# Low parts of the weights on GpSimd in pieces of 256 columns, none from C's last gates to the merge, and two one-column products with pointer scalars

## The chip, the cores and the metric

The kernel runs on one core of a Trainium2 chip. The metric is the device time of one execution in microseconds (us). The engines are called as the profile calls them: PE is TensorE (PEld its weight loads), DVE is VectorE, ACT is ScalarE, POOL is GpSimd, and SP is SyncE, which issues the DMA transfers.

## The reference

A bidirectional encoder trunk of two layers for 512 positions of width 1024, all in float32. Each layer normalises its input, projects it once, and feeds three token mixers: A (grouped attention with axial rotary positions), B (differential attention) and C (multi-head latent attention). Their outputs are merged by gates, projected and added back. A squared-ReLU MLP of width 4096 follows.

```python
for l in range(DEPTH):
    p = _split_columns(rms_norm(x, ln1) @ w_in[l])        # A, B, C and three gates of 1024 columns
    ys = gqa_axial(...), diff_attention(...), mla(...)    # 512 columns each
    merged = sum(sigmoid(gate[n]) * (ys[n] @ w_branch[l, n]) for n in range(3))
    x = x + merged @ w_out[l]
    x = x + relu(rms_norm(x, ln2) @ w_ff1[l]) ** 2 @ w_ff2[l]
return rms_norm(x, final_g)

# inside diff_attention, for each head: two softmaxes and
p = p[0] - lam * p[1]
```

## The kernel before

Every large product is made of three products of split operands. A weight tile of 128 rows and up to 1024 columns comes from memory raw (`wr`). ACT rounds it to the high part `wh` (L60), and DVE or POOL makes the low part `wl` = raw - high (L63). TensorE then multiplies high by high, high by low and low by high; of a weight tile, each 128 columns serve one step of the accumulation, with its three products one behind the other. There are two buffers of raw tiles (`NWR`) and three each of high and low parts (`NW`). A raw tile is free for SyncE's next fetch when its low part is made. All low parts count up `nw`, and `nw % 5 < POOLW` sends one to POOL, else to DVE:

```python
e = t.nc.gpsimd if t.nw % 5 < t.POOLW else t.nc.vector
e.tensor_tensor(wl, self.raw, wh.bitcast(F32), op=ALU.subtract)
```

`POOLW` is 1 (`P0`) from a layer's start, 5 (`PA`) from A's attention on, so that all low parts are POOL's, and 0 (`PF`) from `stat2`, which is called in the first MLP product once output products and their sums are made.

`Trunk.plan` lists a layer's work as (cost, function, weights). `run` goes through that list, fetches weights 8 plan-us ahead (`AHEAD_F`) and splits them 3 plan-us ahead (`AHEAD_S`). `weave` spreads filling work (projections, gates, branch products) between the units of an attention by their costs; `defer` and `tick` call follow-up steps (transposes, products with the values) when a due time on the plan's clock has come. So a low part stands in its engine's queue where the plan's clock put it, and each engine runs its queue in order.

The stages of layer 0 in the trace, in us from the span's start: start and A's projection 0 to 65, A's attention 65 to 180 (with B's projections as filler), B's 180 to 300 (with gates and branch products of A), C's projection 300 to 360, C's attention 360 to 543, the merge 543 to 571, the output product 571 to 613, and the MLP 613 to 963. Layer 1 repeats them from 963 on, and the last norm ends at 1929.

The places that matter below:

- `probs` makes a 128 x 512 block of scores, takes the row maximum (L512, `mx`), in A and C scales it with `scale`, a 128 x 1 column (L516), and lets ACT make the exponential (L517). B's probabilities combine two of them: the second sum's reciprocal (L672) is multiplied by the negated lambda `nlam` and the first sum (L673, both 128 x 1), and L674 adds the two blocks.
- `rsqrt` (L169 to L180) is a chain of small DVE operations; L621 adds the halves of a rotated B block, and L784 makes a part of C's rotated key.
- `branch` (L920, L922) of the third mixer scales a gate `gc`, adds it to the running sum `mg` on DVE, and splits the sum into high (ACT, L150) and low part (DVE, L157): the merged tile `mp`, from which `out` is multiplied. For the second mixer L922 runs on POOL.
- L528 transposes the probabilities on PE, and L532 takes their low part. L155 and L157 make low parts of activations.

Of the kernel before, what the change touches and what calls it, by code (L numbers as in the profile page):

```python
# [10 lines left out]
F32 = mybir.dt.float32  # L11
# [3 lines left out]
ALU = mybir.AluOpType  # L15
# [26 lines left out]
class Weight:  # L42
# [11 lines left out]
    def get(self):  # L54
        if self.parts is None:
            self.fetch()
            t = self.t
            wh = t.p.tile([128, self.cols], F32R, tag="wh", name="wh", bufs=t.NW)
            wl = t.p.tile([128, self.cols], F32R, tag="wl", name="wl", bufs=t.NW)
            t.nc.scalar.copy(wh, self.raw)  # L60
            t.nw += 1
            e = t.nc.gpsimd if t.nw % 5 < t.POOLW else t.nc.vector
            e.tensor_tensor(wl, self.raw, wh.bitcast(F32), op=ALU.subtract)  # L63
            self.parts = wh, wl
        return self.parts


class Trunk:
# [24 lines left out]
    def run(self, plan):  # L93

        at, ws = 0.0, []
        for c, _, w in plan:
            ws += [(at, x) for x in w]
            at += c
        t0, kf, kg = self.t, 0, 0
        for c, f, _ in plan:  # L100
            now = self.t - t0
            while kf < len(ws) and ws[kf][0] <= now + self.AHEAD_F:
                ws[kf][1].fetch()
                kf += 1
            while kg < len(ws) and ws[kg][0] <= now + self.AHEAD_S:
                ws[kg][1].get()
                kg += 1
            self.tick(self.t)
            f()
            self.t += c  # L110

    @staticmethod
    def weave(att, fill):

        tf = sum(x[0] for x in fill)
        done, k, r = 0.0, 0, []
        for i, a in enumerate(att):
            r.append(a)
            while k < len(fill) and done + fill[k][0] / 2 <= tf * (i + 1) / len(att):
                r.append(fill[k])  # L120
                done += fill[k][0]
                k += 1
        return r + fill[k:]
# [382 lines left out]
    def probs(self, mms, scale=None, z=None):  # L506

        nc = self.nc
        s = self.ps("S", "sc")
        self.mm(s, mms)  # L510
        m = self.small("mx", 1, 8)
        nc.vector.tensor_reduce(m, s, axis=AX.X, op=ALU.max, negate=True)  # L512
        p = self.p.tile([128, 512], F32, tag="p", name="p", bufs=self.NP)
        z = self.small("z", 1, 8) if z is None else z
        if scale is not None:
            nc.vector.tensor_tensor(m, m, scale, op=ALU.mult)  # L516
        nc.scalar.activation(p, s, AF.Exp, bias=m, scale=1.0 if scale is None else scale, accum_out=z)  # L517
        return p, z

# [56 lines left out]
    def att_a(self):  # L576
        self.y = {}

        def probs(h, qt):
            g, j, e = h // 4, h // 2, h % 2  # L580
            q = slice(qt * 128, (qt + 1) * 128)
            G, K = self.want(self.aG, j), self.want(self.aK, g)
            i = qt * 4 + h % 4
            p, z = self.probs([(G[:, e, q], K[:, 0]), (G[:, e, q], K[:, 1])], self.aR[g][:, i : i + 1])
            self.normalise(p, z)
            return p

        def vt(h):
            o = 64 * (h % 2)
            return lambda k: self.aV[h // 4][:, k, o : o + 128]  # L590

        return self.attend(probs, vt, self.finish_plain("a"), 1.3)
# [63 lines left out]
    def att_b(self, l):  # L656
        nc = self.nc

        def probs(h, qt):

            if h == 0 and qt == 0:
                self.b_stack(0)
            if qt == 0 and h < 7:
                self.b_stack(h + 1)
            q = slice(qt * 128, (qt + 1) * 128)
            Q, K = self.bs["q"][h], self.bs["k"][h]
            if h % 2 == 0 and qt == 0:
                self.bz[h // 2] = self.p.tile([128, 8], F32, tag="bz", name="bz", bufs=2)
            i = 2 * qt + h % 2
            p0, z0 = self.probs([(Q[0:96, 0, q], K[0:96, 0])], z=self.bz[h // 2][:, i : i + 1])  # L670
            p1, z1 = self.probs([(Q[0:96, 1, q], K[0:96, 1])])
            nc.vector.reciprocal(z1, z1)  # L672
            nc.vector.scalar_tensor_tensor(z1, z1, self.nlam, z0, op0=ALU.mult, op1=ALU.mult)  # L673
            nc.vector.scalar_tensor_tensor(p0, p1, z1, p0, op0=ALU.mult, op1=ALU.add)  # L674
            return p0

        def vt(h):
            o = 128 * (h % 2)
            return lambda k: self.bV[h // 2][:, k, o : o + 128]

        def finish(j, yt):
            sq = self.tmp("bsq")
            nc.scalar.activation(sq, yt, AF.Square)
            self.defer(2.0, lambda: sums(j, yt, sq))

        def sums(j, yt, sq):
            ps = self.ps("T", "bss", (128, 8))
            for tt in range(4):
                self.mm(ps[:, 2 * tt : 2 * tt + 2], [(sq[:, tt * 128 : (tt + 1) * 128], self.blk)])
            v, rs = self.small("bv", 8), self.small("brs", 8)  # L690
            z = self.bz[j]
            nc.vector.scalar_tensor_tensor(z, z, EPS, z, op0=ALU.mult, op1=ALU.mult)
            nc.vector.scalar_tensor_tensor(v, ps, 1.0 / 64, z, op0=ALU.mult, op1=ALU.add)
            self.rsqrt(rs, v, 8)
            R = self.tmp("bR", (128, 4, 2, 64))
            nc.vector.tensor_copy(R, rs.rearrange("p (t h) -> p t h", h=2).unsqueeze(3).to_broadcast([128, 4, 2, 64]))
            self.defer(3.0, lambda: scale(j, yt, R))

        def scale(j, yt, R):
            T = self.ps("T", "bT")  # L700
            Rf = R.rearrange("p t h f -> p t (h f)")
            for tt in range(4):
                nc.tensor.transpose(T[:, tt * 128 : (tt + 1) * 128], Rf[:, tt], self.ident)
            nc.vector.scalar_tensor_tensor(yt, yt, self.gsub, T, op0=ALU.mult, op1=ALU.mult)
            y = self.s4("yb")
            self.split(y, yt)
            self.ys["b"][j] = y

        return self.attend(probs, vt, finish, 1.3)


# [163 lines left out]
    def att_c(self):  # L875
        def probs(h, qt):
            q = slice(qt * 128, (qt + 1) * 128)
            Q, K = self.cQ[h], self.cK[h]
            p, z = self.probs([(Q[:, 0, q], K[:, 0]), (Q[:, 1, q], K[:, 1]), (Q[:, 1, q], self.krl[:, h % 2])],
                              self.rq[:, qt : qt + 1])  # L880
            self.normalise(p, z)
            return p

        def vt(h):
            o = 128 * (h % 2)
            return lambda k: self.cV[h // 2][:, k, o : o + 128]

        return self.attend(probs, vt, self.finish_plain("c"), 1.5)
# [46 lines left out]
    def plan(self, l):  # L935
        nc = self.nc
# [24 lines left out]
        weave = self.weave  # L961
        kv = self.a_kv(l)
        r = [(0, begin, [])] + kv + [(0, stat, [])] + self.a_q(l, 0) + self.a_q(l, 1)
# [6 lines left out]
        att = self.att_b(l)  # L970
# [4 lines left out]
        att = self.att_c()  # L975
        g2 = [x[0] for x in gb[2]]
        r += weave(att[:8], self.c_pair(l, 1) + gates(1, 0, 4))
        r += weave(att[8:16], self.c_pair(l, 2) + self.c_v(l, 1) + gates(1, 4, 8))
        r += weave(att[16:24], self.c_pair(l, 3) + g2[:3])
        r += weave(att[24:], g2[3:7]) + g2[7:]  # L980
        r += [(0, self.tick, [])] + [x[1] for x in gb[2]]
        xs, x2, st2, ff = [], [], {}, []

# [231 lines left out]
```

## Time and profile before

| | us |
|---|---|
| median of 3 runs (lowest to highest) | 1930.42 (1930.24 to 1931.06) |
| the profiled execution's own time | 1930.61 |
| its span | 1928.8 |
| PE busy | 1850.0 |
| DVE busy | 1228.1 |
| ACT busy | 917.0 |
| POOL busy, of which low parts | 427.9, 326.7 |
| mean granted TensorE clock | 0.988 |

The profiled execution stands 0.2 us above the median, so its rows can be set against it directly. A group's row has line, engine, operation, output and inputs with shapes, count, busy time, mean duration of one, then the engine's idle time ahead of it and what ended it. A row of the waits names the waiting instruction, what released it, and total, count and longest in us. PEclk of 0.50 means half of the full TensorE clock in that stretch.

### The profile page before, as it was taken

The numbers are of one execution on the slowest core, as the hardware profiler recorded it, in microseconds if no ns is written. First come the engines' busy times: TensorE is split into PE (matmuls) and PEld (weight loads), VectorE is DVE, ScalarE is ACT, GpSimd is POOL, SyncE is SP. The second block draws the span as 40 slices with busy tenths as digits, with TensorE's granted clock in tenths as the row PEclk, the third lists the DMA queues.
The fourth block names the chain that finished last, engine by engine and source line by source line (L and its number), as shares of the span: only waits on it lengthen the run. The fifth ranks groups of instructions, "written<-read, shape, count | busy, mean of one in ns | idle before, by whom it ended". The sixth has DMA issues, their size and how long they took to land.

```text
span 1928.8 us, 26145 instructions
## 1 busy us (share of the span) xinstructions
PE 1850.0 (96%) x9848; PEld 1572.5 (82%) x9848; DVE 1228.1 (64%) x2234; ACT 917.0 (48%) x1658; POOL 427.9 (22%) x260
## 2 busy tenths in 40 slices
PE   8999989999989999999999999999999999999997
PEld 8888777778878888888898887777888788888886
DVE  7888888756665443444477989796575654334434
ACT  5476656755534331343245766556565334213322
POOL 4211233344235000000141112324432430000000
PEclk9999999999999999999999999999999999999998
DMA  4213331222132332323321133213221432233231
GB/s 159 76 36 84 96 96 54 83 81 89 50 136 89 98 99 91 97 97 114 115 94 60 40 94 109 77 45 97 84 91 39 147 99 90 96 99 98 99 99 66
DMA packets 63150, 171.83 MB, mean 89 GB/s; under 512 B 9520, under 2 KB 14000, under 8 KB 63024
## 3 DMA queue, kind: packets, MB, share of 16 engines
q1 hardware_dynamic: 63024, 170.16, 28.1%
q8 instruction: 78, 1.28, 0.3%
q14 instruction: 48, 0.39, 0.1%
HBM read 149.15 MB, written 4.19 MB: 80 GB/s over the span
## 4 chain that ended last, share of the span: by engine, by line
PE 68%; DVE 11%; ACT 4%; issue 1%; SPq 1%; DMA 1%; POOL 0%; DVEq 0%; ACTq 0%; POOLq 0%
PE ff L147 36%; PE gate L147 10%; PE out L147 4%; PE br L147 3%; PE sc L147 3%; PE pv L147 3%; PE pT L528 2%; PE c_rank L147 2%; PE tm L234 2%; DVE mg L922 1%; DVE mx L512 1%; ACT p L517 1%; DVE mx L516 1%; SPq L160 1%; DVE p L674 1%
## 5 line engine op out<-in xcount | busy, mean ns | idle before, releaser
L60 ACT CAST wh<-wr 128x1024 fp32r<-128x1024 f32 (+5 forms) x310 | 292.0, 942 | 630.0 <-PE ff L147 434.1
L63 POOL TENSOR_TENSOR wl<-wr,wh 128x1024 fp32r<-128x1024 f32 (+4 forms) x170 | 326.7, 1923 | 736.0 <-ACT wh L60 723.7
L63 DVE TENSOR_TENSOR wl<-wr,wh 128x1024 fp32r<-128x1024 f32 (+2 forms) x140 | 171.9, 1228 | 281.2 <-ACT wh L60 281.1
L147 PE MATMUL ff<-ff,wh 128*128 128x512 f32 (+1 forms) x1056 | 317.5, 383 | 0.0
L147 PE MATMUL ff<-xg,wh 128*128 128x512 f32 x1024 | 315.6, 389 | 0.0
L147 PE MATMUL gate<-xg,wh 128*128 128x512 f32 x768 | 242.5, 394 | 1.1 <-DVE c_K L155 1.1
L147 PEld LDWEIGHTS ff<-ff,wh 128*128 128x128 f32 x1056 | 196.3, 188 | 38.8
L147 PEld LDWEIGHTS ff<-xg,wh 128*128 128x128 f32 x1024 | 192.1, 188 | 39.9
L234 PE MATMUL tm<-wh,xg 128*128 128x256 f32 x1024 | 203.8, 290 | 0.0
L147 PE MATMUL ff<-ff,wl 128*128 128x512 f32 (+1 forms) x528 | 202.0, 383 | 0.0
L147 PE MATMUL ff<-xg,wl 128*128 128x512 f32 x512 | 199.4, 389 | 0.0
L512 DVE TENSOR_REDUCE mx<-sc 128x1 f32<-128x512 f32 x256 | 173.8, 683 | 35.7 <-PE sc L147 35.2
L147 PEld LDWEIGHTS gate<-xg,wh 128*128 128x128 f32 x768 | 143.4, 189 | 30.5 <-PE pv L147 1.5
L234 PEld LDWEIGHTS tm<-wh,xg 128*128 128x128 f32 x1024 | 165.6, 193 | 0.2
L277 POOL TENSOR_TENSOR acc<-acc,sq 128x512 f32<-128x512 f32 x15 | 24.6, 1641 | 625.2 <-ACT sq L275 625.2
L147 PE MATMUL gate<-xg,wl 128*128 128x512 f32 x384 | 151.1, 394 | 0.0
L532 DVE TENSOR_TENSOR pt<-pT,pt 128x512 fp32r<-128x512 f32 x192 | 131.4, 686 | 25.1 <-ACT pt L531 24.1
L234 PE MATMUL tm<-wl,xg 128*128 128x256 f32 x512 | 145.6, 284 | 0.0
L531 ACT CAST pt<-pT 128x512 fp32r<-128x512 f32 x192 | 112.0, 584 | 65.4 <-PE pT L528 64.2
L528 PE MATMUL pT<-ident,p 128*128 128x128 f32 x768 | 116.9, 275 | 13.2 <-DVE p L674 8.6
L528 PEld LDWEIGHTS pT<-ident,p 128*128 128x128 f32 x768 | 91.3, 141 | 39.0 <-issue 17.6
L147 PEld LDWEIGHTS ff<-ff,wl 128*128 128x128 f32 x528 | 99.2, 188 | 19.3
(240 smaller groups left out, 3175.1 us busy)
## 6 DMA issues: line engine op xcount, KB each, us to landing
wr<-w SPq DMA_DIRECT2D x234, 512.0 KB, 3.5
wr<-w SPq DMA_DIRECT2D x52, 256.0 KB, 2.6
b_sq<-b_f SPq DMA_DIRECT2D x96, 64.0 KB, 2.5
b_sk<-b_f SPq DMA_DIRECT2D x96, 64.0 KB, 2.0
x<-xT SPq DMA_DIRECT2D x8, 256.0 KB, 5.5
c_Q<-c_qr SPq DMA_DIRECT2D x32, 64.0 KB, 2.5
c_K<-c_krf SPq DMA_DIRECT2D x16, 128.0 KB, 4.0
x<-xT SPq DMA_DIRECT2D x4, 512.0 KB, 5.8
```

The source lines that it names most:

```text
L60: t.nc.scalar.copy(wh, self.raw)
L63: e.tensor_tensor(wl, self.raw, wh.bitcast(F32), op=ALU.subtract)
L147: self.nc.tensor.matmul(out, l, r, start=(i == 0), stop=(i == n - 1))
L160: self.nc.sync.dma_start(dst.bitcast(F32), src.bitcast(F32))
L234: self.nc.tensor.matmul(ps, l, r, start=(u == 0 and i == 0 and tt % 2 == 0), stop=(u == 1 and tt % 2 == 1 and i == len(p) - 1))
L277: e.tensor_tensor(st[d % 2], st[d % 2], sq, op=ALU.add)
L512: nc.vector.tensor_reduce(m, s, axis=AX.X, op=ALU.max, negate=True)
L516: nc.vector.tensor_tensor(m, m, scale, op=ALU.mult)
L517: nc.scalar.activation(p, s, AF.Exp, bias=m, scale=1.0 if scale is None else scale, accum_out=z)
L528: nc.tensor.transpose(T[:, k], p[:, k * 128 : (k + 1) * 128], self.ident)
L531: nc.scalar.copy(h[:, :, q], T)
L532: nc.vector.tensor_tensor(lo[:, :, q], T, h[:, :, q].bitcast(F32), op=ALU.subtract)
```

## The change

Three edits. POOL makes a low part in pieces of 256 columns, one instruction each, while DVE still makes it whole. The products of L516 and L673 become `tensor_scalar` with one or two 128 x 1 operands as pointer scalars. And `POOLW` is set to 0 ahead of the last two gates of the third mixer, instead of in `stat2` alone (which still sets it).

```diff
@@ Weight.get
-            e = t.nc.gpsimd if t.nw % 5 < t.POOLW else t.nc.vector
-            e.tensor_tensor(wl, self.raw, wh.bitcast(F32), op=ALU.subtract)
+            e, n = (t.nc.gpsimd, 256) if t.nw % 5 < t.POOLW else (t.nc.vector, 1024)
+            for o in range(0, self.cols, n):
+                q = slice(o, min(o + n, self.cols))
+                e.tensor_tensor(wl[:, q], self.raw[:, q], wh[:, q].bitcast(F32), op=ALU.subtract)
@@ probs
-            nc.vector.tensor_tensor(m, m, scale, op=ALU.mult)
+            nc.vector.tensor_scalar(m, m, scale, None, op0=ALU.mult)
@@ att_b, probs
-            nc.vector.scalar_tensor_tensor(z1, z1, self.nlam, z0, op0=ALU.mult, op1=ALU.mult)
+            nc.vector.tensor_scalar(z1, z1, self.nlam, z0, op0=ALU.mult, op1=ALU.mult)
@@ plan
-        r += weave(att[24:], g2[3:7]) + g2[7:]
+        r += weave(att[24:], g2[3:6])
+        r += [(0, lambda: setattr(self, "POOLW", self.PF), [])] + g2[6:]
```

In the changed kernel line numbers are three or four higher: L63 becomes L66, L157 L160, L277 L280, L418 L421, L739 L742, L920 L923, L922 L925, L995 L999.

Since a weight is split ahead of its use, the gate before last is already split when `POOLW` changes. What passes from POOL to DVE is, in each layer, one gate, the 8 branch weights of the third mixer (512 columns), the 8 output weights and the first 4 of the MLP. Over both layers POOL has 170 instructions of low parts before (100 of 1024 columns, 52 of 512, 18 smaller), and 398 after (390 of 256 columns, 8 of 128).

POOL's queue in A's and B's attention of the first layer (`a_t` is a rotated block of A, `c_sq` a square in C's projection), before:

```order
L63 TENSOR_TENSOR wl<-wr,wh 128x1024
L418 TENSOR_TENSOR a_t_633<-a_tq 128x1024
L63 TENSOR_TENSOR wl<-wr,wh 128x1024 x8
L63 TENSOR_TENSOR wl<-wr,wh 128x512
L63 TENSOR_TENSOR wl<-wr,wh 128x1024
```

The same place after:

```order
L66 TENSOR_TENSOR wl<-wr,wh 128x256 x4
L421 TENSOR_TENSOR a_t_636<-a_tq 128x1024
L66 TENSOR_TENSOR wl<-wr,wh 128x256 x90
L742 TENSOR_TENSOR c_sq<-c_sq 128x512
L66 TENSOR_TENSOR wl<-wr,wh 128x256 x6
```

Each whole weight stands as four pieces, each of 512 columns as two, in the old place.

POOL's queue from the last sum of the second mixer (`mg<-mg,gz`) through C's last gates, the merge and the output product (`acc` sums squares for the norm) of layer 0, before:

```order
L922 TENSOR_TENSOR mg<-mg,gz 128x512
L63 TENSOR_TENSOR wl<-wr,wh 128x1024 x7
L63 TENSOR_TENSOR wl<-wr,wh 128x512 x8
L63 TENSOR_TENSOR wl<-wr,wh 128x1024 x6
L277 TENSOR_TENSOR acc<-acc,sq 128x512
```

After:

```order
L925 TENSOR_TENSOR mg<-mg,gz 128x512
L66 TENSOR_TENSOR wl<-wr,wh 128x256 x27
L280 TENSOR_TENSOR acc<-acc,sq 128x512 x3
L283 TENSOR_TENSOR acc<-acc 128x512
```

The branch and output weights are gone from POOL.

DVE's queue at the end of the merge of layer 0 (`gc` gate times branch product, `mg` the running sum, `mp` the low part of the merged tile, `x` the residual sum), before:

```order
L920 SCALAR_TENSOR_TENSOR gc<-gc,br 128x512
L922 TENSOR_TENSOR mg<-mg,gc 128x512
L157 SCALAR_TENSOR_TENSOR mp<-mg,mp 128x512
L920 SCALAR_TENSOR_TENSOR gc<-gc,br 128x512
L922 TENSOR_TENSOR mg<-mg,gc 128x512
L157 SCALAR_TENSOR_TENSOR mp<-mg,mp 128x512
L995 TENSOR_TENSOR x<-out,x 128x512
```

After:

```order
L66 TENSOR_TENSOR wl<-wr,wh 128x1024
L160 SCALAR_TENSOR_TENSOR mp<-mg,mp 128x512
L923 SCALAR_TENSOR_TENSOR gc<-gc,br 128x512
L66 TENSOR_TENSOR wl<-wr,wh 128x1024
L925 TENSOR_TENSOR mg<-mg,gc 128x512
L923 SCALAR_TENSOR_TENSOR gc<-gc,br 128x512
L160 SCALAR_TENSOR_TENSOR mp<-mg,mp 128x512
L925 TENSOR_TENSOR mg<-mg,gc 128x512
L66 TENSOR_TENSOR wl<-wr,wh 128x1024
L160 SCALAR_TENSOR_TENSOR mp<-mg,mp 128x512
L999 TENSOR_TENSOR x<-out,x 128x512
```

Three whole low parts of output weights now stand ahead of the last merged tile, and ahead of them six of 512 columns for the branch products. The orders of SP, PE and ACT stay nearly as they were.

## The prediction

> **What bounds the kernel now.** I read the page first: busy times, then the chain that ended last. Columns: busy us, share of the span, instructions.
>
> ```profile
> PE 1850.0 (96%) x9848; PEld 1572.5 (82%) x9848; DVE 1228.1 (64%) x2234; ACT 917.0 (48%) x1658; POOL 427.9 (22%) x260
> PE 68%; DVE 11%; ACT 4%; issue 1%; SPq 1%; DMA 1%; POOL 0%; DVEq 0%; ACTq 0%; POOLq 0%
> ```
>
> TensorE (PE) is busy for 96% of the span. No product is added or removed, so the change is worth what it does to PE's waits and to its clock. Hence the list of waits, PE's rows (total us, times, longest):
>
> ```profile
> PE sc L147 <- ACT p L517: 11.0, 6, 2.7
> PE out L147 <- ACT mp L150: 8.9, 4, 3.1
> PE pT L528 <- DVE p L674: 8.6, 8, 2.1
> PE tp L263 <- DVE b_t L621: 8.4, 6, 2.1
> ...
> PE pT L528 <- DVE p L522: 3.7, 5, 1.5
> ...
> PE bc L147 <- DVE pt L532: 3.1, 2, 1.5
> ```
>
> Those six rows are 43.7 us. Each ends at VectorE (DVE) or at ScalarE behind it, so I looked at the timeline in front of them (start, us, operation). First a scaling of a row maximum, then a rope sum:
>
> ```profile
> 463.42 2.39 POOL L63 TENSOR_TENSOR wl<-wr,wh 128x1024 fp32r<-128x1024 f32 x1 [4.46 <-ACT wh L60]
> 463.95 1.88 DVE L516 TENSOR_TENSOR mx<-mx,c_rq 128x1 f32<-128x1 f32 x1
> ...
> 465.77 1.30 POOL L922 TENSOR_TENSOR mg<-mg,gz 128x512 f32<-128x512 f32 x1
> ...
> 78.78 2.35 POOL L63 TENSOR_TENSOR wl<-wr,wh 128x1024 fp32r<-128x1024 f32 x1 [4.62 <-ACT wh L60]
> 78.86 2.55 DVE L621 TENSOR_TENSOR b_t<-b_r 128x256 f32<-128x256 f32 x1
> ...
> 81.56 1.75 PE L263 MATMUL tp<-ident,b_t 128*128 128x128 f32 x8 [2.09 <-DVE b_t L621]
> ```
>
> One element per partition takes 1.88 us, because GpSimd (POOL) started a low part 0.53 us earlier: both end within 0.03 us of each other (465.81, 465.83). The DVE operation has two inputs in SBUF and waits for POOL's operation to end; it then runs at the boundary although POOL's next one starts at 465.77. So a DVE stall is as long as what is left of one POOL instruction, and shorter instructions bound it. At 78.86 the stall reaches PE, which waits 2.09.
>
> A second cost follows the long waits: the granted clock (last three columns: clock, DMA share, GB/s; before them us, then busy us of PE, PEld, DVE, ACT, POOL):
>
> ```profile
> 81.80:85.20 3.40, 3.40 (x18) 3.40 (x17) 2.75 (x8) 1.85 (x4) 0.00 (x0) 0.50 0.54 157
> ...
> 569.90:576.70 6.80, 6.05 (x14) 4.45 (x15) 3.60 (x4) 2.92 (x4) 2.38 (x1) 0.50 0.65 260
> 1034.10:1037.50 3.40, 3.40 (x16) 3.10 (x15) 2.23 (x6) 1.63 (x4) 0.00 (x0) 0.50 0.38 143
> 1221.80:1225.20 3.40, 3.40 (x13) 2.91 (x12) 2.66 (x6) 2.00 (x5) 1.20 (x1) 0.50 0.01 2
> ...
> 1518.80:1525.60 6.80, 3.79 (x9) 2.44 (x9) 3.98 (x4) 2.42 (x4) 2.81 (x2) 0.50 0.98 374
> sum 30.60, PE 26.84 PEld 21.65 DVE 21.74 ACT 14.75 POOL 6.39; mean PE 3.83 PEld 3.09 DVE 3.11 ACT 2.11 POOL 0.91
> ```
>
> In these stretches (the sum is over seven; two are left out) PE runs at half clock right behind a wait of about 2 us or more. Half of 26.84 us of work, 13.4, is lost there.
>
> **The change, part by part.** The sum goes against the profiled execution's own 1930.61; the median of the runs is 0.2 lower.
>
> ```profile
> L63 POOL TENSOR_TENSOR wl<-wr,wh 128x1024 fp32r<-128x1024 f32 x100 | 239.9, 2399 | 497.6 <-ACT wh L60 485.4 <-PE sc L147 7.6 <-PE br L147 4.5
> ...
> L63 POOL TENSOR_TENSOR wl<-wr,wh 128x256 fp32r<-128x256 f32 x8 | 6.0, 751 | 16.9 <-ACT wh L60 16.9
> ...
> L63 DVE TENSOR_TENSOR wl<-wr,wh 128x1024 fp32r<-128x1024 f32 x134 | 165.8, 1237 | 277.9 <-ACT wh L60 277.9
> ...
> L922 DVE TENSOR_TENSOR mg<-mg,gc 128x512 f32<-128x512 f32 x16 | 27.5, 1719 | 0.5
> ```
>
> *Pieces of 256 columns.* A whole weight takes 2.40 us on POOL, four pieces 4 x 0.751 = 3.00. The longest stall falls from 2.40 to 0.75. By PE's rows:
>
> Rope sums (8.4 in 6), by the durations of that line (ns, least/median/longest):
>
> ```profile
> L621 DVE TENSOR_TENSOR b_t<-b_r x8: 424/2301/2557, 66.1 to 1104.7; 128x256 f32<-128x256 f32 x8
> ```
>
> A stall of 2.30 - 0.42 = 1.88 becomes at most 0.75, 1.13 less in each of 6: 6.8. Its half-clock stretches (81.80, 1034.10) go: (3.40 + 3.40)/2 = 3.4. Together 10.2.
>
> Scores behind the softmax (11.0 in 6). Four are large, two of each kind below:
>
> ```profile
> 240.93 4.22 POOL L63 TENSOR_TENSOR wl<-wr,wh 128x512 fp32r<-128x512 f32 x2 [7.54 <-ACT wh L60]
> 241.51 1.26 DVE L176 TENSOR_TENSOR rst<-rsy 128x8 f32<-128x8 f32 x1
> 242.80 2.38 DVE L177 TENSOR_TENSOR rst<-rst,rsh 128x8 f32<-128x8 f32 x1
> ...
> 1216.23 2.59 DVE L784 TENSOR_TENSOR c_kr<-c_r 128x512 f32<-128x512 f32 x1
> ...
> 1220.94 0.50 PE L147 MATMUL sc<-b_sk,b_sq 96*128 96x512 f32 x1 [2.16 <-ACT p L517]
> ```
>
> L784 is one operation behind one POOL instruction: 2 x 1.65 = 3.3, and the stretch at 1221.80 goes (1.7). L176 to L180 are a chain of tiny operations (the reciprocal square root), and each can meet a piece of its own: POOL's two weights there become four pieces, 3.0 us, against stalls of 1.26 + 2.38 less 0.15 each, 3.3. I take the 0.3, twice, 0.6, and no clock. Together 5.6.
>
> Transposes of B's probabilities (8.6 in 8): between nothing and three quarters. I take a quarter, 2.2, since several small operations follow each other ahead of L674 and the second can meet the next piece, as in the chain.
>
> *Pointer scalars.* They bear on C's and A's transposes (3.7) and the diagonal's products (3.1), whose long waits have a stalled L516 ahead. The trace has no one-element operation with one tensor and pointer scalars inside a POOL operation. The nearest is L374, with one tensor and a constant:
>
> ```profile
> 23.62 0.45 POOL L360 TENSOR_TENSOR tabs<-rope,rows 128x128 f32<-128x128 f32 x1
> 23.71 0.15 DVE L374 TENSOR_SCALAR nlam<-nlam 128x1 f32<-128x1 f32 x1
> ...
> L516 DVE TENSOR_TENSOR mx<-mx,c_rq 128x1 f32<-128x1 f32 x64 | 30.8, 482 | 1.6
> ```
>
> L374 runs in 0.15 inside a POOL operation. The bounds are 0.15 and, if a pointer makes it wait, half a piece more, 0.52. I take the first, since both read one tensor: L516 falls from a mean of 482 ns to its free 0.15 (64 x 0.33 = 21 us of DVE time in C alone, mostly covered by PE's other work). Of the 6.8 I take 60%, 4.1; the operation behind L516 can still meet a piece.
>
> The Trainium skill speaks against this part: "SBUF — State Buffer", section "Who interferes with whom", says that tensor_scalar can take the ports shared with GpSimd, and "VectorE: DVE Perf Modes", section "What auto-detection actually checks", admits a single SBUF source whose outermost non-unit sizes are even or equal, as 1 and 1 are. By that rule the stalls would stay at about half a piece, 0.37, some 5 us of the gain here would not come, and the time would be about 1912; the row of L374 disagrees, so I keep mine.
>
> *No low parts on POOL from C's last gates on.* Per layer 8 branch weights (512 columns), and whole ones of one gate, 8 of the output and 4 of the feed-forward, pass to DVE: 26 x 1.237 + 16 x 0.62 (half of a whole one) = 42 us over both layers. The merge:
>
> ```profile
> 543.00:571.00 28.00, 23.17 (x100) 18.30 (x98) 23.45 (x24) 10.19 (x16) 13.68 (x8) 0.98 0.45 151
> 571.00:613.00 42.00, 42.00 (x174) 34.21 (x174) 23.03 (x18) 15.95 (x22) 22.98 (x11) 0.93 0.37 115
> ...
> 567.38 2.55 DVE L922 TENSOR_TENSOR mg<-mg,gc 128x512 f32<-128x512 f32 x1
> ...
> 570.65 1.52 PE L147 MATMUL out<-mp,wh 128*128 128x512 f32 x2 [3.11 <-ACT mp L150]
> ```
>
> There DVE is busy 23.45 of 28, of which the eight L922 stall (1719 - 690) x 8 = 8.2 (0.69 is what its neighbours of 512 columns take). In their place come six branch low parts, 6 x 0.62 = 3.7, and three of output weights ahead of the last merged tile, 3 x 1.24 = 3.7: 0.8 net if all is one chain. If DVE's new work falls into its 4.5 us of idle time, the merge ends up to 4.4 earlier, PE's whole wait. I take 2.0 per layer, 4.0, and half of the two stretches' (6.05 + 3.79)/2 = 4.9 of clock, 2.5. Together 6.5. In the output stage (571 to 613) PE is full and DVE busy 23 of 42, stalls included: its share of the 42 us costs nothing there. If that cover were gone, PE would wait 1.24 a weight, 16 times, 20 us.
>
> The Trainium skill would price the clock otherwise: "TensorE: Matmul & The Clock Gate", section "HAM oscillation", allows idle gaps up to about 3.4 us. By that rule no clock is won back and the time is 7.6 us higher (3.4 + 1.7 + 2.5), about 1914.5; the trace has 0.50 at 81.80 behind a wait of 2.09, and disagrees.
>
> *Costs.* A raw tile is released 0.6 us later per whole weight (3.00 - 2.40), and SyncE's next fetch starts later. Only the casts that end on a DMA feel it:
>
> ```profile
> ACT wh L60 <- DMA wr<-w: 6.5, 5, 2.0
> ```
>
> 5 x 0.6 = 3.0. The 74 whole weights left on POOL keep it busy 44 us longer; 43.7 us of PE waits came with 327 of low parts, and stalls are a third as long: 43.7/3 x 44/327 = 2.0. Costs 5.0. PE's low products now wait piece by piece, but the first piece ends 1.65 before the whole did.
>
> Sum: 10.2 + 5.6 + 2.2 + 4.1 + 6.5 - 5.0 = 23.6; 1930.6 - 23.6 = 1907.0, against the median 1906.8; I say 1907. Bounds: all six rows and all the clock, 57.1, give 1873.5; nothing in the merge and half of the other 22.3, less 5.0, gives 1924.4.
>
> **The rivals.**
> Handed on: the stalls were covered, or DVE, now with 42 us more, is late with the next operation in line. For it: C's L516 stalls for 21 us, and PE's transposes wait 3.7 of them. 1924.4 as just worked out.
> All recovered: for it, the stalls end exactly with POOL's instructions; against it, the chain at L176 and a full DVE in the merge. Near 1880.
> Slower: late weights in the attentions.
>
> ```profile
> 381.20 2.40 POOL L63 TENSOR_TENSOR wl<-wr,wh 128x1024 fp32r<-128x1024 f32 x1 [8.28 <-ACT wh L60]
> ...
> 385.80 0.39 PE L147 MATMUL gate<-xg,wl 128*128 128x512 f32 x1
> ```
>
> A low part ends at 383.60 and PE needs it at 385.80, slack 2.2. If POOL pauses at each boundary while DVE's waiting operation (0.69) runs, four pieces take 3.00 + 4 x 0.69 = 5.8, 3.4 more than now and 1.2 past the slack. It decides from (2.2 - 0.6)/0.69 = 2.3 pauses a weight. Some 46 gate weights (24 a layer less one) x 1.2 = 55, less 23.6, is +31: 1962. Against it: POOL started at 465.77 while L516 ran, and PE needs the first piece alone at first.
> No change: every shorter stall meets a second one, and the two clocks stay: 1930.
>
> **How the numbers follow.** The likeliest, 1894 to 1917, has 0.56; handed on (1917 to 1926.5) 0.20; all recovered (under 1894) 0.14; slower 0.05; no change 0.05. 0.2%, 3.9 us, is about what a measurement of this kernel tells from no change. Faster 0.90, same 0.05, slower 0.05. The range leaves out slower and no change, 0.10, the top sixth of handed on, 0.03, and the lowest third of recovered, 0.05: 1881 to 1925.
>
> **What would show it.** L516 at 0.15 to 0.25 in both groups; L621 under 1.2; no DVE stall over 0.8 in the attentions; clock 1.0 where 81.8, 1034.1 and 1221.8 stood at 0.50; PE's wait at `out` under 6 us; POOL busy near 390 (427.9 - 26 x 2.40 - 16 x 1.2 + 74 x 0.6). I am wrong if DVE's low parts appear among PE's waits in merge or output stage, if L516 still ends with POOL's pieces, or if the casts' DMA waits exceed 10 us.

## The result and the profile after

The changed kernel takes 1881.78 us (median of 4 runs, 1880.87 to 1884.26) against 1930.33 before: a ratio of 0.975, 95% interval 0.9733 to 0.9767. It is 48.6 us faster, where 23.4 were forecast. The time lies 0.8 us inside the low end of the stated range (1881 to 1925), in the case that the prediction called all recovered and gave 0.14. That it lies in the range at all is luck: the sum missed more than half of the gain.

The first lines of the page, as before:

```profile
span 1880.7 us, 26473 instructions
...
PE 1835.7 (98%) x9848; PEld 1564.2 (83%) x9848; DVE 1177.7 (63%) x2276; ACT 916.5 (49%) x1658; POOL 394.8 (21%) x488
...
PE 82%; DVE 10%; ACT 5%; issue 2%; DMA 1%; POOL 0%; SPq 0%; DVEq 0%; ACTq 0%; POOLq 0%
```

PE runs the same 9848 instructions in 14.3 us less busy time (1850.0 before). All rows of PE's waits together sum to 36.7 us, from 71.6. Waits 34.9 and busy time 14.3 make 49.2, and the span is 48.1 shorter, so these two account for the result. The rows of PE's waits:

```profile
PE tm L250 <- ACT wh L60: 6.8, 1, 6.8
PE pT L531 <- DVE p L525: 4.0, 4, 1.8
PE sc L150 <- ACT p L520: 3.9, 5, 1.2
PE tp L266 <- DVE a_G L158: 3.0, 2, 2.1
...
PE pT L531 <- DVE p L677: 2.5, 4, 0.9
```

Of the six rows of before, three are gone: the rope sums, the merge's `out`, the diagonal's products behind `pt`. At the rope sums' own products two waits of 0.47 are left, behind an exponential (the row `tp` <- ACT `p`, 0.9). The score row fell from 11.0 to 3.9, and the row of B's transposes from 8.6 to 2.5. But B's last units run beside C's projection, and there PE's waits at B's transposes are put down to VectorE's `c_rq`, `c_sq` and `c_qr`. With these rows B's transposes wait 9.0 before and 5.4 after. C's transposes did not gain (3.7 to 4.0). The first row, 6.8, is one wait at the start that no edit touches.

What was in front of those waits, by groups (busy, mean ns, idle before). Before, the means were 268 ns (A) and 482 ns (C) for L516, 482 for L673 and 1719 for L922:

```profile
L66 POOL TENSOR_TENSOR wl<-wr,wh 128x256 fp32r<-128x256 f32 x390 | 290.3, 774 | 523.4 <-ACT wh L60 504.7 <-DMA b_sk<-b_f 13.1 <-DMA wr<-w 5.4
...
L676 DVE TENSOR_SCALAR z<-z,nlam,bz 128x1 f32<-128x1 f32 x64 | 17.2, 269 | 1.0
L519 DVE TENSOR_SCALAR mx<-mx,c_rq 128x1 f32<-128x1 f32 x64 | 13.5, 211 | 1.4
...
L925 DVE TENSOR_TENSOR mg<-mg,gc 128x512 f32<-128x512 f32 x16 | 11.0, 686 | 0.1
L66 DVE TENSOR_TENSOR wl<-wr,wh 128x512 fp32r<-128x512 f32 x16 | 11.0, 685 | 0.5 <-ACT wh L60 0.5
```

L925, the old L922, takes 0.69 us in every case, as its neighbours do. The two pointer scalars never wait, by the durations of all 192 (least, median, longest, in ns). Unhindered they take some 0.05 us longer than the old forms did (medians of 214 and 270 against 159 and 219):

```profile
L519 DVE TENSOR_SCALAR mx<-mx,a_R x64: 194/214/217, 79.8 to 1093.8; 128x1 f32<-128x1 f32 x64
L519 DVE TENSOR_SCALAR mx<-mx,c_rq x64: 194/214/217, 345.7 to 1437.5; 128x1 f32<-128x1 f32 x64
...
L676 DVE TENSOR_SCALAR z<-z,nlam,bz x64: 257/270/277, 178.3 to 1261.8; 128x1 f32<-128x1 f32 x64
...
L624 DVE TENSOR_TENSOR b_t<-b_r x8: 424/650/926, 65.8 to 1073.3; 128x256 f32<-128x256 f32 x8
```

The longest rope sum is 0.93 us instead of 2.56, which is 0.42 of its own and less than one piece.

The windows of merge and output product, from C's first branch product to the MLP's first product, of both layers, before and then after:

```profile
537.50:612.50 75.00, 70.17 (x297) 56.36 (x296) 48.38 (x43) 27.67 (x40) 36.63 (x20) 0.95 0.38 121
1489.10:1562.80 73.70, 69.13 (x297) 55.53 (x296) 48.34 (x43) 27.60 (x40) 36.73 (x20) 0.95 0.37 124
```

```profile
522.60:588.20 65.60, 65.60 (x291) 53.88 (x290) 42.83 (x58) 27.88 (x40) 6.76 (x4) 1.00 0.43 144
1448.80:1514.50 65.70, 65.70 (x290) 53.83 (x289) 42.70 (x58) 28.02 (x40) 6.77 (x4) 1.00 0.44 144
```

PE is now busy for the whole of both stretches and the clock is 1.00. They are 9.4 and 8.0 us shorter, 17.4 together. Of this 1.8 is not a gain: before, seven products with C's values, 0.9 us in each layer, stand inside the stretch, and after they stand ahead of it. So 15.5 us are gained. DVE's busy time fell too (48.4 to 42.8), though it has 15 instructions more.

### The profile page after: what moved, and what is told of

Read it like the earlier page. It is cut to its first block, busy times and chain, and to the rows that moved or that the text cites. A ratio compares the mean times of both kernels' runs of the same rounds, so it can differ in the third digit from the quotient of the medians.

```text
span 1880.7 us, 26473 instructions
## 1 busy us (share of the span) xinstructions
PE 1835.7 (98%) x9848; PEld 1564.2 (83%) x9848; DVE 1177.7 (63%) x2276; ACT 916.5 (49%) x1658; POOL 394.8 (21%) x488
## 4 chain that ended last, share of the span: by engine, by line
PE 82%; DVE 10%; ACT 5%; issue 2%; DMA 1%; POOL 0%; SPq 0%; DVEq 0%; ACTq 0%; POOLq 0%
PE ff L150 37%; PE gate L150 12%; PE br L150 6%; PE tm L237 6%; PE out L150 5%; PE sc L150 4%; PE pv L150 4%; PE pT L531 3%; PE c_rank L150 2%; DVE mx L515 1%; ACT p L520 1%; DVE p L677 1%; ACT c_K L153 1%; PE tm L250 1%; ACT c_Q L153 1%
## 5 line engine op out<-in xcount | busy, mean ns | idle before, releaser
L66 POOL TENSOR_TENSOR wl<-wr,wh 128x256 fp32r<-128x256 f32 (+1 forms) x398 | 293.8, 767 | 523.4 <-ACT wh L60 504.7
L66 DVE TENSOR_TENSOR wl<-wr,wh 128x1024 fp32r<-128x1024 f32 (+3 forms) x182 | 214.6, 1179 | 294.6 <-ACT wh L60 294.5
L280 POOL TENSOR_TENSOR acc<-acc,sq 128x512 f32<-128x512 f32 x15 | 25.1, 1675 | 804.7 <-ACT sq L278 804.7
```

The costliest lines, as they stand in the source:

```text
L66: e.tensor_tensor(wl[:, q], self.raw[:, q], wh[:, q].bitcast(F32), op=ALU.subtract)
L280: e.tensor_tensor(st[d % 2], st[d % 2], sq, op=ALU.add)
```

## The experiments

Times are medians. Differences are to the kernel before as measured beside them (1931.39 for e1 to e4, 1932.47 for e5 to e8, 1930.41 for e9 to e12).

| run | edit | us | difference |
|---|---|---|---|
| e1_pieces | pieces of 256 alone | 1889.57 | -41.8 |
| e2_scalars | pointer scalars alone | 1925.64 | -5.8 |
| e3_move | `POOLW` moved alone | 1917.47 | -13.9 |
| e4_pieces_move | pieces and move | 1884.90 | -46.5 |
| e12_pieces_scalars | pieces and pointer scalars | 1886.37 | -44.0 |
| e9_again | all three, the changed kernel | 1882.41 | -48.0 |
| e5_half_pieces | changed, pieces of 512 | 1896.17 | -36.3 |
| e6_eighth_pieces | changed, pieces of 128 | 1880.99 | -51.5 |
| e7_all_on_dve | changed, nearly all low parts on DVE | 1885.35 | -47.1 |
| e8_branch_only | move for the branch weights alone | 1921.25 | -11.2 |
| e10_merge_double | changed, branch low parts on DVE made twice | 1886.61 | -43.8 |
| e11_mixed | piece sizes and engines by stage | 1875.59 | -54.8 |

### One edit at a time

The edits are those of the diff above, one of them each.

> Pieces of 256 columns alone; L516 and L673 stay tensor_tensor, POOLW is set as before. Theory one (each edit gives back PE's waits behind the stalls it shortens, and the clock behind those waits; nothing is handed on): rope, score and transpose waits nearly go (some 33 us, as the first two thirds of the changed kernel gained), and in the merge the stall of L922 falls from 1.0 to under 0.4 us each, so about 10 of the merge's 16 come too: 1888. Rival (the prediction's terms): 10.2 + 5.6 + 2.2 less 5.0 = 13 us, 1917.

Measured 1889.57, -41.8 (ratio 0.9782, interval 0.9767 to 0.9797): theory one. Pieces alone are most of the result, and the prediction's terms for them (13 us) fell short by 29. The merge and output stretches that took 148.7 us together take 139.2 here, 9.6 less, with the same products in them. Two rows of PE's waits stay large:

```profile
PE pT L531 <- DVE p L525: 5.5, 7, 1.9
PE pT L531 <- DVE p L677: 5.3, 8, 1.5
```

The second fell from 8.6; L673 and L516 still wait in front of it, for a piece at a time (up to 0.97 and 1.13 us). The first grew from 3.7: two of its seven waits, 1.9 and 1.8, have another cause, found below under the size of a piece.

> Pointer scalars alone. Theory one: L516 at 0.21 and L673 at 0.27 us in every case, the two waits of 1.5 at the diagonal's products and those at C's transposes (1.5 each) go, part of the 8.6 at B's transposes; 5 to 9 us, about 1923. Rival one (handed on: the operation behind L516 has two SBUF inputs or is of even size and meets the same whole 2.4-us instruction): within 2 us of before, 1929. Rival two (a pointer scalar waits like a tensor): L516 and L673 keep durations above 1 us, 1930.

Measured 1925.64, -5.8 (0.9953 to 0.9977): theory one. L516 is 191 to 217 ns in all 128 cases, while POOL's operations are still whole; a pointer scalar of one element doesn't wait. Of the 192 pointer scalars 34 begin and end within one POOL instruction, where before none of them did. The place that took 1.88 in the prediction's first timeline (463.95):

```profile
463.35 2.40 POOL L63 TENSOR_TENSOR wl<-wr,wh 128x1024 fp32r<-128x1024 f32 x1 [4.46 <-ACT wh L60]
...
463.94 0.21 DVE L516 TENSOR_SCALAR mx<-mx,c_rq 128x1 f32<-128x1 f32 x1
```

But part is handed on, as the first rival has it. PE's waits of this kernel:

```profile
PE sc L147 <- ACT p L517: 11.0, 6, 2.7
PE out L147 <- ACT mp L150: 9.3, 4, 3.1
PE tp L263 <- DVE b_t L621: 8.2, 6, 2.1
...
PE pT L528 <- DVE rsy L171: 4.0, 2, 2.0
PE pT L528 <- DVE p L674: 3.7, 4, 0.9
...
PE pT L528 <- DVE c_rq L756: 1.6, 2, 0.8
```

The wait behind L522 has fallen from 3.7 to 0.4, and the diagonal's behind `pt` (3.1) is off the list. B's transposes did not gain: their row of 8.6 has become 4.0 + 3.7, and with those behind `c_rq` (1.6), `c_sq` (1.2) and `c_qr` (0.7) they wait 11.2, against 9.0 before. The first three rows don't move: they stand behind other operations.

> POOLW set to 0 ahead of C's last two gates, alone. Theory one: the merge and the output product gain what they gained in the changed kernel, 8.7 + 7.2 = 15.9 us, and nothing elsewhere: 1914.5. Rival (the prediction's term): DVE's added low parts take back most, 6.5 us, 1924.

Measured 1917.47, -13.9 (0.9915 to 0.9948): theory one, with 1917.5 between 1914.5 and the rival's 1924. The stretch of merge and output is 65.65 and 65.61 us long, as in the changed kernel. PE is busy throughout here too:

```profile
539.00:604.50 65.50, 65.50 (x289) 53.78 (x288) 42.79 (x58) 27.90 (x40) 6.77 (x4) 1.00 0.44 145
```

> Pieces and the move, L516 and L673 as before. Theory one: pieces already bound the stalls of L516 and L673 to 0.77 us, so the pointer scalars add little: 3 us above the changed kernel, 1885. Rival (the edits add up): as many us above it as the pointer scalars alone bring, 7: 1889.

Measured 1884.90, -46.5 (0.9745 to 0.9774): theory one. The edits don't add up: -41.8, -5.8 and -13.9 make 61.5, all three together 48. Once the stalls are short, the other two have less to take. The pointer scalars add 1.5 to 2 us to this kernel, which the intervals don't tell from nothing.

> Pieces and pointer scalars, POOLW set as before. Theory one (with pieces the stall of L922 in the merge is down to 0.4, so that the move is worth 5 here and not the 14 that it is worth alone): 5 us above the changed kernel, 1887. Rival (the edits add): 14 above, 1896.

Measured 1886.37, 4.0 above the changed kernel measured beside it (e9): theory one. L925 with pieces of 256 still on POOL, and the wait that stays:

```profile
L925 DVE TENSOR_TENSOR mg<-mg,gc 128x512 f32<-128x512 f32 x16 | 17.2, 1072 | 0.6
...
PE out L150 <- ACT mp L153: 2.7, 2, 1.5
```

A stall of 0.39 in the mean, and PE waits 2.7 instead of 8.9.

### The size of a piece

```diff
-            e, n = (t.nc.gpsimd, 256) if t.nw % 5 < t.POOLW else (t.nc.vector, 1024)
+            e, n = (t.nc.gpsimd, 512) ...      # e5; 128 in e6
```

> The changed kernel with pieces of 512 columns on GpSimd (1.32 us each instead of 0.77). Theory one (a stall is bounded by one piece, and PE's waits and half-clock stretches follow the longest stall): waits between the 36.7 us of the changed kernel and the 61 of the move alone, some 45, one or two half-clock stretches back: 1890 to 1896. Rival (any cut is enough, because a second operation can run at each boundary): within 3 us of the changed kernel, 1882 to 1885.

Measured 1896.17, -36.3 (0.9802 to 0.9831): theory one, at the upper end. All PE's waits are 45.2, as expected, and the clock is 0.993 of full speed in the mean, against 0.997. A cut in two isn't enough.

> The changed kernel with pieces of 128 columns (by the rows of 1024, 512 and 256 some 0.46 us each, 3.7 a weight). Theory one: stalls fall once more, PE's waits by about 5 us: 1876 to 1879. Rival (late weights: more boundaries, a low part takes 1.3 us longer than whole and pauses at eight boundaries, and the raw tile is late): PE waits at gate or branch for POOL's pieces, or ACT's casts wait for DMA and PE behind them, 1885 or more.

Measured 1880.99, -51.5 (ratio 0.9719 to 0.9751, which overlaps the changed kernel's): between the two, nearer theory one. A piece takes 496 ns, eight 4.0 us, 1.6 longer than the whole. All PE's waits are 34.3 instead of 36.7, and the gain over 256 columns is 3.5 us at most.

Something grows against it. ACT's casts wait longer for raw tiles: 6.5 us before, 21.1 in the changed kernel, 30.8 here. The row of the changed kernel:

```profile
ACT wh L60 <- DMA wr<-w: 21.1, 8, 3.8
```

This is the prediction's term for raw tiles that come free later, and it reaches PE at C's transposes. The changed kernel in front of the longest of them:

```profile
446.40 0.74 POOL L66 TENSOR_TENSOR wl<-wr,wh 128x256 fp32r<-128x256 f32 x1 [4.64 <-ACT wh L60]
447.10 1.29 POOL L925 TENSOR_TENSOR mg<-mg,gz 128x512 f32<-128x512 f32 x1
448.35 5.27 POOL L66 TENSOR_TENSOR wl<-wr,wh 128x256 fp32r<-128x256 f32 x7
...
450.69 0.33 SPq L52 DMA_DIRECT2D wr<-w  x1
...
454.85 1.05 ACT L60 CAST wh<-wr 128x1024 fp32r<-128x1024 f32 x1 [3.51 <-DMA wr<-w]
...
458.74 0.78 ACT L520 ACTIVATE p<-sc,mx,c_rq 128x512 f32<-128x512 f32 x1
...
459.84 0.48 DVE L525 TENSOR_SCALAR p<-p,z 128x512 f32<-128x512 f32 x1
...
460.47 0.63 PE L531 MATMUL pT<-ident,p 128*128 128x128 f32 x4 [1.83 <-DVE p L525]
```

A sum of the second mixer stands in POOL's queue between the first and the second piece, so this low part takes from 446.40 to 450.67 instead of 2.4 us. SyncE fetches the next raw tile only then, ACT waits 3.51 us for it, and the exponential stands behind that cast in ACT's queue. No VectorE operation is stalled between the cast and PE's wait. The same place in the other kernels bears it out. With 512 columns the cast waits 3.0 to 3.1 and PE 1.3 to 1.4, with 256 columns 3.5 and 1.8, with 128 columns 4.1 and 2.4; with the low parts on VectorE (e7, next) 0.2 and 0.45. PE waits for no high or low part itself, here or in the changed kernel, apart from 6.6 to 6.8 us at the start and one of 0.3 here. ACT's row as a whole also grows without pieces (17.0 in e7), so not all of it is their doing.

### Is GpSimd needed?

```diff
-        self.P0, self.PA, self.PF = 1, 5, 0
+        self.P0, self.PA, self.PF = 1, 0, 0
```

> The changed kernel with POOLW at 0 from A's attention on, so that VectorE makes nearly all low parts and GpSimd's pieces hardly exist. Theory one (GpSimd still pays: VectorE gets 74 whole weights of 1.24 us and 36 of 512 columns more, 114 us, mostly in stages where it is already 70 to 90% busy): slower than the changed kernel by 10 to 40 us, 1892 to 1922, with PE waiting for DVE's softmax operations. Rival (the stalls were the only cost of sharing, and DVE's idle time takes the low parts): 1870 to 1880.

Measured 1885.35, -47.1 (0.974 to 0.977). Neither theory: with 99% of the low parts on VectorE, the kernel is only 1 to 2 us behind the changed one (-48.0 and -48.6), which the intervals don't tell from nothing, and 5 us short of the rival. DVE is busy 1251.5 us, 74 more than in the changed kernel and 23 more than before. So GpSimd's help with whole low parts cost far more than it saved: before, which also lacks the pointer scalars, is 47 us slower. With pieces the help saves hardly anything. By these two kernels the gain of the change is the end of the stalls, however it is had. The longest waits here are at the scores (the row of 3.9 in the changed kernel); what stands in front of them was not taken apart:

```profile
PE sc L150 <- ACT p L520: 6.0, 4, 2.8
```

### The merge

```diff
-        r += weave(att[24:], g2[3:7]) + g2[7:]
-        r += [(0, self.tick, [])] + [x[1] for x in gb[2]]
+        r += weave(att[24:], g2[3:6])
+        r += [(0, lambda: setattr(self, "POOLW", self.PF), [])] + g2[6:]
+        r += [(0, self.tick, [])] + [x[1] for x in gb[2]][:7]
+        r += [(0, lambda: setattr(self, "POOLW", self.PA), [])] + [gb[2][7][1]]
```

> The kernel before, with POOLW at 0 from C's last two gates to the last but one branch product and back at 5 then: of a layer the gate, the branch weights and two of twelve further weights go to VectorE, ten output and MLP weights stay on GpSimd whole. Theory one (the gain of the move is the end of L922's stall in the merge): as the move alone within 3 us, 1917 to 1920. Rival (much of the gain comes from the output product, where L157 of the residual, 1.6 us each under GpSimd's low parts, falls to 0.8): 1923 to 1928.

Measured 1921.25, -11.2 (0.9928 to 0.9958): by the difference to before, within 3 us of the move alone (-13.9), so theory one at its edge; by the time itself, between the two. The stretches of merge and output take 67.33 and 67.10 us, with those seven products ahead of them here too. So 12.5 of the 15.5 us are the merge's, that is L922's stall; the output product and what little of it meets the last branch give the other 3.

> The changed kernel with each of the 16 branch low parts of 512 columns that VectorE makes in C's end and the merge made twice, 0.69 us more each, 11 us in all. Theory one (VectorE's four operations take 2.7 us a chunk, as long as PE's branch product, so the added low parts fit exactly and nothing more does): of 0.69 a chunk about 0.5 is not covered, PE waits 2 to 4 us per layer at out, with half clock behind it or not: 4 to 12 us above the changed kernel. Rival (the merge has slack beyond that, because output products and gate 7 fill PE): within 2 us of it.

The edit repeats VectorE's instruction where a weight has 512 columns.

Measured 1886.61, 4.2 above the changed kernel measured beside it: theory one at its lower end, with the wait at another place. 4.1 of the 11 us reach PE, at the branch products themselves, and the rest is still covered:

```profile
PE br L152 <- DVE wl L68: 3.1, 2, 1.5
...
PE br L152 <- ACT wh L60: 1.0, 2, 0.5
```

So the merge has some slack beyond what the change puts there, but not 11 us. It is seen in the changed kernel's timeline, one chunk of the merge (start, us):

```profile
533.99 0.69 DVE L923 SCALAR_TENSOR_TENSOR gc<-gc,br 128x512 f32<-128x512 f32 x1 [0.23 <-PE br L150]
...
534.59 0.69 DVE L66 TENSOR_TENSOR wl<-wr,wh 128x512 fp32r<-128x512 f32 x1
535.19 0.69 DVE L160 SCALAR_TENSOR_TENSOR mp<-mg,mp 128x512 fp32r<-128x512 f32 x1
535.80 0.69 DVE L925 TENSOR_TENSOR mg<-mg,gc 128x512 f32<-128x512 f32 x1
...
536.71 0.69 DVE L923 SCALAR_TENSOR_TENSOR gc<-gc,br 128x512 f32<-128x512 f32 x1 [0.23 <-PE br L150]
```

Four operations start 0.60 apart and VectorE then waits 0.23 for PE: the chunk lasts 2.72 us by PE's branch product, not by VectorE.

### A mix that beats both

The edit, shortened; `PN` takes the place of 256 as the size of a piece, and is 256 from the start:

```diff
+        use = lambda w, n: [(0, lambda: (setattr(self, "POOLW", w), setattr(self, "PN", n)), [])]
+        r += use(self.PA, 128)                              # from A's attention on
         r += weave(self.att_a(), fb[self.FB :] + fb1)
+        r += use(0, 256)                                    # first half of B's attention
         r += weave(att[:16], gates(0, 0, 6))
+        r += use(self.PA, 128)                              # second half, C's projection
         r += weave(att[16:], ...)
+        r += use(self.PA, 256)                              # C's attention
```

> The changed kernel with 128-column pieces on GpSimd from A's attention on, all low parts on VectorE for the first half of B's attention, 128-column pieces again for C's projection, and 256 in C's attention; the rest as changed. Theory one (gains of stages add: the best of each run, 10.9 + 9 + 3.3 + 1.8 + 5.6 and 9.1 + 9 + 4.1 + 1.1 + 4.2): 55 to 59 us under before, 1873 to 1877. Rival (what is left of PE's waits isn't behind GpSimd): within 3 us of the changed kernel.

Measured 1875.59, -54.8 (ratio 0.9694 to 0.9723, clear of the changed kernel's 0.9733 to 0.9762 beside it). It is 6.8 us faster than the changed kernel, theory one. PE's waits sum to 29.3 us. The scores keep 1.4. The largest row behind the one at the start is C's transposes, where the late cast costs two waits of 1.5:

```profile
PE pT L531 <- DVE p L525: 3.5, 4, 1.5
```

## Why the prediction was wrong

The mechanism was right: VectorE waits for the end of GpSimd's instruction, and a shorter instruction bounds the wait. The sign and the places were right too. The sizes were not: the sum gave 23.6 us and 48.6 came. The step that failed most is the merge, where VectorE's added low parts were set against its removed stalls as one chain; the second is the clock. Term by term, in us (waits are PE's rows, before less after):

| term | forecast | measured |
|---|---|---|
| rope sums, waits | 6.8 | 7.5 (8.4 to 0.9) |
| scores, waits | 3.9 | 7.1 (11.0 to 3.9) |
| B's transposes, under all names | 2.2 | 3.6 (9.0 to 5.4) |
| C's transposes and the diagonal, without the late casts | 4.1 | 6.4 (6.8 to 0.4) |
| merge, waits | 4.0 | 8.9 (8.9 to 0) |
| clock | 7.6 | 14.3 (PE busy 1850.0 to 1835.7) |
| costs | -5.0 | -3.6 (late casts, at C's transposes) |
| sum | 23.6 | 44.2, and 5.0 in other rows |

*The merge* (6.5 forecast with its clock, 15.5 measured for merge and output) is the largest step that failed. The prediction set DVE's removed stall, 8.2 a layer, against 7.4 of added low parts, "0.8 net if all is one chain", and took a value between that and PE's whole wait. The chain doesn't exist: e3 and the chunk above show VectorE waiting 0.2 for PE in each chunk, with the low part in it. The three output low parts that stand ahead of the last merged tile in the order were covered too, though one of 512 columns takes 0.69 where 0.62 was reckoned. PE's pace of 2.72 us a chunk and four operations at 0.60 could have been set against each other beforehand: 2.4 is less than 2.72. With the durations of 0.69 it is 2.75, and the merge looks full. The prediction also put the merge under the third edit alone, while pieces alone already win 9.6 of it (e1).

*The clock.* The prediction gave back only half-clock stretches whose wait it removed whole, and half of the merge's. In the changed kernel all eight are gone, also those at 249 and 1256, though waits of 0.9 to 1.2 stay at those places. One new stretch has come, at 69.4 (after: that one, the stretch in which 249 falls, and 1256's):

```profile
69.40:72.80 3.40, 3.40 (x19) 3.40 (x18) 1.70 (x4) 2.14 (x3) 0.71 (x2) 0.50 0.29 107
```

```profile
233.00:241.00 8.00, 6.84 (x36) 5.31 (x35) 7.77 (x19) 4.50 (x11) 2.84 (x5) 1.00 0.53 148
...
1212.00:1215.40 3.40, 2.89 (x14) 2.18 (x15) 3.40 (x8) 1.75 (x4) 1.62 (x2) 1.00 0.17 45
```

So shortened waits were enough at these eight places. Nor did every stretch stand behind its long wait: in the merge they begin at 569.9 and 1518.8, while the waits of 3.1 and 3.0 end at 570.65 and 1522.14. The prediction cited the Trainium skill, "TensorE: Matmul & The Clock Gate", section "HAM oscillation", by which gaps up to about 3.4 us leave the clock alone. The trace disagrees: no wait of before in these places was longer than 3.1 us, and PE's busy time fell by 14.3 us with the same products.

*Handing on.* Scores and B's transposes were discounted by the idea that a chain of small operations meets a piece each. It does at the square-root chain: in the changed kernel L179 and L180 take 0.70 and 0.66 us there, one piece each. Yet PE's wait behind it fell from 2.73 to 1.2, not by 0.3, because row maxima and exponentials of other rows get in between. B's transposes, under all names, wait 5.9 in e1, with pieces alone, and 5.4 in the changed kernel. The scores are at 2.4 without pointer scalars (e1, e4) and at 3.7 and 3.9 with them (e12, the changed kernel). So there the pointer scalars move waits rather than end them, as the rival of handing on says. What they end when they come alone (e2) are the waits of C's transposes and of the diagonal.

*Costs.* The forecast had 3.0 for raw tiles released late and 2.0 for new collisions. The raw tiles cost 3.6, the two waits at C's transposes. That the sizes are near is luck: five casts with 0.6 each were reckoned, and two with 3.5 came, because another operation had got in between the pieces. A new collision has not been found. ACT's waits for transfers rose beyond the 10 us that the prediction named as a sign against itself, to 21.1. The sign was right about a cost, though the other gains were far larger.

The signs it named otherwise came out: L516 at 0.21, no duration over 0.93 at the rope sum, clock 1.00 at the three places, `out` off the list, POOL busy 394.8 against 390. The rival of late weights did not occur: PE waits for no low part of POOL's. Two slips are small: in the bound of 1924.4 the other terms stand as 22.3 and add up to 22.1, and 1.13 was taken off each of the six rope waits, four of which held only 1.05.

Pointer scalars did not wait: 192 cases of at most 0.277 us. The prediction's rule against them (the Trainium skill, "SBUF — State Buffer", section "Who interferes with whom", with "VectorE: DVE Perf Modes", section "What auto-detection actually checks") speaks, in the second, of non-unit sizes. Reading it as met by 1 and 1 went too far: by these runs it does not hold for one column.

## What to carry to other kernels

Where one engine's operations wait for the end of another's instructions, as VectorE's did here, the longest of those instructions is the price; cut it before moving work, or try without the second engine. See what comes free later by the cut: a late buffer went through a fetch, a cast and ScalarE's queue to PE. And price a wait that is shortened, not only one that is removed: the slower clock behind it may go as a whole. A count of an engine's added work says little until it is set against the pace of the one it feeds, with start-to-start times in place of durations.

## What the runs showed of the hardware

A VectorE `tensor_scalar` on one column with pointer scalars runs beside GpSimd (191 to 277 ns in e2, where GpSimd's low parts are whole). A `tensor_scalar` on 16 columns with constants waits. In e2 one of four met a low part and ended with it; the other three take 0.17:

```profile
50.41 2.39 POOL L63 TENSOR_TENSOR wl<-wr,wh 128x1024 fp32r<-128x1024 f32 x1
50.52 2.32 DVE L171 TENSOR_SCALAR rsy<-rsy 128x16 int32<-128x16 int32 x1
```

The half clock isn't set by the length of a wait alone. Before, the same wait of 2.73 us ahead of a score product was followed by half clock in layer 0 (247.3, half from 249.0) and not in layer 1 (1198.9). Thirteen of the fourteen profiles have a wait of 2.1 to 2.3 ahead of a rope product at 69 to 70 us. Behind it the clock is at half in eight of them, the changed kernel's among these, and full in five, among them before. In e1 a wait of 1.33 at 552.0, with one of 0.33 behind it, was enough. The windows behind 1198.9, before, and behind that of e1:

```profile
1198.00:1203.00 5.00, 4.12 (x22) 3.36 (x23) 4.77 (x13) 4.49 (x11) 0.00 (x0) 1.00 0.68 200
```

```profile
553.80:557.20 3.40, 3.40 (x10) 2.63 (x9) 0.77 (x2) 1.88 (x3) 2.67 (x5) 0.51 1.02 392
```

What else decides wasn't tried.
